# Two parts of the conditioning rows at a time beside the last o products, in matmuls of 512 columns

## The chip, the cores and the metric

The kernel runs on one core of one Trainium2 chip. Its engines each take their own list of instructions in order: TensorE (PE in the profile; its weight loads are PEld), VectorE (DVE), ScalarE (ACT), GpSimd (POOL) and SyncE (SP), which here issues the DMAs. Semaphores hold them together. The metric is the device time of one execution in microseconds (us), lower is better.

## The reference

One inference step of a two-layer streaming encoder, for a prompt of 1024 rows and a sample of 32 rows, with width D = 1024. Layer 0 mixes by an mLSTM with 4 heads, layer 1 by chunk-band attention; both have an MLP with a squared ReLU. What matters here is the conditioning: each layer makes six vectors of 1024 entries (shift, scale and gate, twice) from the conditioning vector c of the sequence, and applies them to its rows.

```python
def ada_mod(c, w, b):
    return jax.nn.silu(c) @ w + b
...
sh1, sc1, g1, sh2, sc2, g2 = jnp.split(ada_mod(c, p['w_ada'][l], p['b_ada'][l])[:, None, :], 6, axis=-1)
u = x * (1 + sc1) + sh1
...
x = layer_norm(ALPHA * x + (1 + g1) * y, p['ln_g'][l, 0], p['ln_b'][l, 0])
u = x * (1 + sc2) + sh2
```

w_ada is 1024 x 6144 for each layer. c is a single row for the prompt and one for the sample, so these products have two rows of output and read 4 MB of weights for each of the six parts. The mLSTM mixer ends with an output gate, `h * sigmoid(o_pre)` with `o_pre = u @ w_in[:, 2048:3072]`, and `h @ w_out`.

## The kernel before

The program is written as a sequence of stages on one core, in fp32 with operands split in a high and a low half where a matmul must be exact. Loops are unrolled when the program is built; a scheduler puts the instructions of each engine in a fixed order, with waits on semaphores where data or a buffer has to be free.

Work that is not the stage's own runs beside it as a task: a Python generator that is handed to `flow` (class Flow, lines 47 to 75). The stage calls `flow.tick()` after each of its own pieces, here with 1.0; a task that is marked `fine` is advanced until the waits that it yields have used up the tick. What the task emits then stands behind that piece in the program's order.

The stage that the change touches is the last one of the mLSTM layer: `o_proj([2, 3], after_o)` (line 864), which makes the output gate of heads 2 and 3. For each of three blocks of rows (384, 384 and 288) and each head it makes two products of 24 matmuls (`proj`, 8 blocks of the contraction with three matmuls each), so twelve products, each with a tick behind it. The products' matmuls are the lines 120 to 122 with the tile name o; the gate itself is made on ACT and DVE from the result (lines 450 to 453, 626, 628).

Beside it runs the task `ada_o` (lines 852 to 863). It computes four of the six parts of layer 1's conditioning (shift and scale of both halves of the layer, parts 0, 1, 3 and 4; columns 48, 56, 72 and 80 of the tile ada), which are first used in the next stages' norms. Each part is one call of `ada_rows`:

- `load` (lines 267 to 272): a block of 128 rows of w_ada, 1024 columns, 512 KB, by one DMA on SP. The tile comes from `mk`, the ring of four y buffers that the heads have left. Three loads are issued ahead.
- line 282: for each of the 8 row blocks k four matmuls, one for each quarter q of the columns. The stationary operand is the two conditioning vectors, padded to 32 columns; quarter q goes to the 32 output partitions from 32q on. A matmul in fp32 is two records in the trace, each with a weight load.
- line 286: the 32 x 4 rows of result are copied by ACT from the bank `ada` (one buffer) to a tile sada, from the ring tmp (three buffers).
- lines 288 to 297: they are transposed on PE and added with the bias into ada by DVE.

The yields of `ada_rows` are 2.5 steps ahead of the first block, a step ahead of each other block and ahead of the copy, and three steps ahead of the transposes. `ada_rows` also serves the key and value conditioning (line 1507), there with two parts at once from one tile.

Beside the same products `ada_l0` (line 792) makes parts of layer 0's conditioning on DVE from 512 KB loads of its own; its result needs the bank `ada` too (line 249, adas). The stage that follows loads its accumulators (acc, line 1053) into memory that pool A gives back, then multiplies by w_out_a (tile op_a).

Of the kernel before, what the change touches and what calls it, by code (L numbers as in the profile page):

```python
# [8 lines left out]
F32 = mybir.dt.float32  # L9
# [6 lines left out]
P = 128  # L16
D = 1024
# [60 lines left out]
def trunk_kernel(ctx: ExitStack, tc: tile.TileContext, a, o):  # L78
    nc = tc.nc
# [6 lines left out]
    def raw_tile(shape, name):  # L86
        return ring.tile(shape, F32, tag="raw", name=name, bufs=3)
# [62 lines left out]
    cs = cp.tile([P, KC, 32], F32, name="cs")  # L150
# [8 lines left out]
    def lng(i):  # L159
        return pt1[:, i * KC:(i + 1) * KC]  # L160

    def lnb(i):
        return pt1[:, 32 + i * KC:32 + (i + 1) * KC]
# [3 lines left out]
    def ada_part(l, i):  # L167
        return ada[:, l * 48 + i * KC:l * 48 + (i + 1) * KC, :]
# [18 lines left out]
    def bank(name):  # L187

        bank_n[0] += 1
        return (tpt, nmt, adat, mmt, tpt, nmt, mmt, mmt)[bank_n[0] % 8](name)  # L190
# [67 lines left out]
    wa, wk = a["w_ada"], a["w_ada_kv"]  # L258
    LA = 6 * D * D

    def ada_rows(src, off, gap, bases, step, mk, bank, ahead=1, mk2=None, mkt=None):

        m = len(bases)
        w = m * D // 4
        nm = bases[0]

        def load(k):
            raw = mk([P, m * D], f"rada_{nm}_{k}")
            row = src.ap[-2][0]
            nc.sync.dma_start(raw.rearrange("p (i c) -> p i c", i=m), bass.AP(  # L270
                src.tensor, src.offset + off + k * P * row, [[row, P], [gap, m], [1, D]]))
            return raw
        raws = [load(k) for k in range(ahead)]
        ps = None
        for k in range(KC):
            if k + ahead < KC:
                raws.append(load(k + ahead))
            raw = raws.pop(0)
            yield step if k else 2.5 * step
            ps = ps or bank(f"adap_{nm}")  # L280
            for q in range(4):
                nc.tensor.matmul(ps[32 * q:32 * q + 32, :w], cs[:, k, :], raw[:, q * w:(q + 1) * w],
                                 start=(k == 0), stop=(k == KC - 1))
        yield step
        sb = (mkt or tmp_t)([P, w], f"sada_{nm}")
        nc.scalar.copy(sb, ps[:, :w])
        yield 3 * step
        ps2 = (mk2 or mmD)(f"adat_{nm}")[:, :w]
        for b in range(w // P):
            nc.tensor.transpose(ps2[:, b * P:(b + 1) * P], sb[:, b * P:(b + 1) * P], ident)  # L290
        for i, base in enumerate(bases):
            nq = 4 // m
            nc.vector.tensor_tensor(
                ada[:, base:base + 8, :].rearrange("p (q b) j -> p q b j", q=nq),
                ps2.rearrange("p (b q j) -> p q b j", b=w // P, q=4)[:, nq * i:nq * i + nq, :, 0:2],
                pt2[:, base:base + 8].rearrange("p (q b) -> p q b", q=nq)[:, :, :, None].broadcast_to(
                    [P, nq, 8 // nq, 2]), op=ALU.add)

    def ada_fix(base, parts):

        for i, kind in parts:
            ap = ada[:, base + i * KC:base + (i + 1) * KC, :]
            if kind == "sc":
                nc.vector.tensor_scalar_add(ap, ap, 1.0)
            else:
                nc.vector.tensor_scalar(ap, ap, 1.0, 1.0 / ALPHA, op0=ALU.add, op1=ALU.mult)

    def combine(ni, g, b, sc, sh):

        for cnd in range(2):  # L310
            nc.vector.tensor_mul(comb[:, ni, :, 0, cnd], g, sc[:, :, cnd])
            nc.vector.tensor_mul(comb[:, ni, :, 1, cnd], b, sc[:, :, cnd])
            nc.vector.tensor_add(comb[:, ni, :, 1, cnd], comb[:, ni, :, 1, cnd], sh[:, :, cnd])
# [57 lines left out]
    A = A_cm.__enter__()  # L371
# [480 lines left out]
    def ada_o():  # L852
        def mk(shape, name):
            return A.tile([P, YL], F32, tag="y", name=name, bufs=4)[:, :D]

        def mkt(shape, name):
            return A.tile([P, 384], F32, tag="tmp", name=name, bufs=3)[:, :shape[1]]
        for i in (0, 1, 3, 4):
            yield from ada_rows(wa, LA + i * D, D, (48 + 8 * i,), 0.22, mk, adat, 3, nmt, mkt)
        ada_fix(48, [(1, "sc"), (4, "sc")])  # L860
        combine(1, lng(1), lnb(1), ada_part(1, 1), ada_part(1, 0))
        combine(2, lng(2), lnb(2), ada_part(1, 4), ada_part(1, 3))
    flow.add(ada_o(), fine=True)
    o_proj([2, 3], after_o)
    flow.finish()
# [71 lines left out]
    def mmD(name):  # L937
        return psum["p"].tile([P, 512], F32, tag="mm", name=name, bufs=psum["n"])
# [567 lines left out]
    def ada_early():  # L1506
        yield from ada_rows(wk, 0, D, (96, 104), 2.9, wc_tile, ada_bank)
        ada_fix(96, [(1, "sc")])
# [170 lines left out]
    for ti, pr in ((2, 0), (2, 1), (2, 2), (1, 0), (1, 1), (1, 2), (2, 3), (1, 3), (0, 3), (0, 2), (0, 1), (0, 0)):  # L1679
# [8 lines left out]
        for fc in (2 * pr, 2 * pr + 1):  # L1688
            g, r = fc // 2, 2 * (fc % 2)
            gp, e = g // 2, g % 2  # L1690
            ps = mmD(f"q_{fc}_{t0}")
            proj(ps[:, :n], n, ws[pr], fc % 2, lambda hl, k: UQ[ti][:, hl, k])
            for hd in range(2):
                for off, m, cnd in segs(t0, n):
                    if cnd == 0:
                        dst = QOT[ti][:, e, gp, 0:m // 64, (r + hd) * 64:(r + hd + 1) * 64]
                        src = ps[64 * hd:64 * hd + 64, off:off + m].rearrange("p (c i) -> p c i", i=64)
                    else:
                        dst = qo(16)[:, e, gp, (r + hd) * 32:(r + hd + 1) * 32]
                        src = ps[64 * hd:64 * hd + 64, off:off + m]  # L1700
# [17 lines left out]
    for i in range(4):  # L1718
        raw = raw_tile([P, 2, 512], f"raw_kv{i}")
# [356 lines left out]
```

## Time and profile before

| What | Value |
|---|---|
| median of 3 runs | 2340.04 us (2337.47 to 2340.95) |
| the profiled execution | 2338.54 us |
| its span, first to last instruction | 2336.8 us |
| granted TensorE clock over the span | 0.996 |
| bytes read from HBM, written | 329.65 MB, 95.46 MB |

In the views of the profile that follow, a row of a timeline has the start (us from the span's start), the time taken, the engine, the line of the kernel, the operation, output<-inputs by the program's tile names, the shape and the count; in square brackets stands how long the engine was idle before it, and what ended that. A row of groups has the busy time and the mean of one instruction in ns, then the idle time before. "SPq" is the issuing of DMAs by SyncE. A row of windows has the stretch, its length, the busy time of each engine with the number of its instructions, the granted clock, the DMA engines' busy share and GB/s. Records of matmuls overlap, so their distances from start to start tell more than their durations.

### The profile page before, as it was taken

How to read it: one execution, taken by the hardware profiler on the slowest of the kernel's cores; microseconds unless marked ns; L12 is line 12 of the kernel's file. 1: busy time of each engine (PE TensorE's matmuls, PEld its weight loads, DVE VectorE, ACT ScalarE, POOL GpSimd, SP SyncE). 2: the span in 40 equal slices, each digit the busy share in tenths (PEclk: the TensorE clock that was granted, in tenths of full speed). 3: DMA queues.
4: the chain of work that ended last, by engine and by line, in shares of the span. 5: the costliest groups of instructions: out<-in, count | busy, mean ns of one | idle time of the engine just before them, and what ended most of it. 6: DMA issues, size and time to landing. Idle time of an engine off the chain costs nothing. (4 is left out here: it accounts for less than half of the span.)

```text
span 2336.8 us, 44003 instructions
## 1 busy us (share of the span) xinstructions
PE 2279.9 (98%) x17266; PEld 2158.1 (92%) x17266; DVE 1823.1 (78%) x3480; ACT 1205.5 (52%) x2278; POOL 150.7 (6%) x309
## 2 busy tenths in 40 slices
PE   7999999999999999999999999999999999999997
PEld 5999998898899999999999877779999999999997
DVE  4899987686788888977886677755788888896777
ACT  4554445337844444333776766653784444433343
POOL 0111100000000000000000034420000000000021
PEclk9999999999999999999999999999999999999999
DMA  9422337747566679857641330042456667976753
GB/s 319 131 84 89 95 97 239 243 155 261 192 223 224 223 242 345 278 181 234 223 157 58 104 75 2 1 134 59 142 195 225 224 221 250 369 258 194 246 167 126
DMA packets 292703, 425.63 MB, mean 182 GB/s; under 512 B 17796, under 2 KB 174872, under 8 KB 291472
## 3 DMA queue, kind: packets, MB, share of 16 engines
q1 hardware_dynamic: 281648, 402.27, 52.9%
q10 hardware_dynamic: 10848, 20.55, 2.4%
q8 instruction: 136, 2.23, 0.4%
q14 instruction: 71, 0.58, 0.1%
HBM read 329.65 MB, written 95.46 MB: 182 GB/s over the span
## 5 line engine op out<-in xcount | busy, mean ns | idle before, releaser
L951 PE MATMUL dP<-t_P_None,w_P_None 128*128 128x256 f32 (+1 forms) x1280 | 365.3, 285 | 0.0
L949 PE MATMUL dP<-t_P_None,w_P_None 128*128 128x256 f32 (+1 forms) x1280 | 363.3, 284 | 0.3 <-DVE acd L1454 0.3
L950 PE MATMUL dP<-t_P_None,w_P_None 128*128 128x256 f32 (+1 forms) x1280 | 361.4, 282 | 0.0
L949 PEld LDWEIGHTS dP<-t_P_None,w_P_None 128*128 128x128 f32 x1280 | 241.2, 189 | 0.6 <-issue 0.5
L950 PEld LDWEIGHTS dP<-t_P_None,w_P_None 128*128 128x128 f32 x1280 | 241.0, 188 | 0.0
L951 PEld LDWEIGHTS dP<-t_P_None,w_P_None 128*128 128x128 f32 x1280 | 240.4, 188 | 0.0
L958 ACT CAST t_P_None<-rt_P_None 128x1056 fp32r<-128x1056 f32 x80 | 86.2, 1079 | 223.6 <-PE dP L951 165.1
L949 PE MATMUL e<-opB,wea 128*128 128x272 f32 (+1 forms) x512 | 146.4, 286 | 6.0 <-DVE sv L1224 3.2
L951 PE MATMUL dP<-t_P,w_P 128*128 128x256 f32 (+1 forms) x512 | 146.8, 287 | 0.1
L949 PE MATMUL dP<-t_P,w_P 128*128 128x256 f32 (+1 forms) x512 | 146.8, 287 | 0.0
L950 PE MATMUL dP<-t_P,w_P 128*128 128x256 f32 (+1 forms) x512 | 146.3, 286 | 0.0
L949 PE MATMUL uP<-opT,wb 128*128 128x264 f32 x512 | 145.7, 285 | 0.0
L951 PE MATMUL e<-opB,wea 128*128 128x272 f32 (+1 forms) x512 | 145.5, 284 | 0.0
L951 PE MATMUL uP<-opT,wb 128*128 128x264 f32 x512 | 145.5, 284 | 0.0
L950 PE MATMUL uP<-opT,wb 128*128 128x264 f32 x512 | 145.2, 284 | 0.0
L950 PE MATMUL e<-opB,wea 128*128 128x272 f32 (+1 forms) x512 | 145.0, 283 | 0.0
L959 DVE TENSOR_TENSOR t_P_None<-rt_P_None,t_P_None 128x1056 fp32r<-128x1056 f32 x80 | 100.2, 1253 | 45.7 <-ACT t_P_None L958 45.4
L958 ACT CAST wb<-rup 128x1024 fp32r<-128x1024 f32 x32 | 33.6, 1050 | 176.2 <-DVE rup L1177 176.2
L949 PEld LDWEIGHTS e<-opB,wea 128*128 128x128 f32 x512 | 96.2, 188 | 10.7 <-ACT sv L1222 4.3
L1158 ACT ACTIVATE h<-h 128x528 f32<-128x528 f32 x96 | 61.6, 641 | 71.9 <-DVE h L1271 71.9
L950 PEld LDWEIGHTS e<-opB,wea 128*128 128x128 f32 x512 | 96.2, 188 | 1.7 <-issue 1.7
L951 PEld LDWEIGHTS dP<-t_P,w_P 128*128 128x128 f32 x512 | 97.3, 190 | 0.4 <-DVE w_P L959 0.4
(419 smaller groups left out, 7492.1 us busy)
## 6 DMA issues: line engine op xcount, KB each, us to landing
rt_P_None<-h_d SPq DMA_DIRECT2D x80, 528.0 KB
rw_P_None<-in_w_down_dram SPq DMA_DIRECT2D x80, 512.0 KB
rada<-in_w_ada_dram SPq DMA_DIRECT2D x72, 512.0 KB
rup<-in_w_up_dram SPq DMA_DIRECT2D x64, 512.0 KB
rw_P<-in_w_down_dram SPq DMA_DIRECT2D x48, 512.0 KB
h_d<-h SPq DMA_DIRECT2D x30, 792.0 KB
rea<-in_w_up_dram SPq DMA_DIRECT2D x64, 256.0 KB
h_d<-t SPq DMA_DIRECT2D x30, 528.0 KB
```

Source lines behind the costliest of these rows:

```text
L949: nc.tensor.matmul(ps, wh, xh, start=start, stop=False)
L950: nc.tensor.matmul(ps, wh, xl, start=False, stop=False)
L951: nc.tensor.matmul(ps, wl, xh, start=False, stop=stop)
L958: nc.scalar.copy(op[:, 0], src)
L959: nc.vector.tensor_sub(op[:, 1], src, raw32(op[:, 0]))
L1158: nc.scalar.activation(dst, dst, AF.Relu)
```

## The change

`ada_o` now calls `ada_rows` twice instead of four times, each time for two neighbouring parts (0 and 1, then 3 and 4). A new argument `parts` gives it the weights of the two parts. A row block is then two tiles of 128 x 1024, each by a load of its own from the same ring of four y buffers, with one row block loaded ahead. The four matmuls of a row block have 512 columns each: quarters 0 and 1 read the first tile's halves, quarters 2 and 3 the second's. The step is 0.44 instead of 0.22. The copy sada has 512 columns and takes a y buffer instead of a tmp buffer. The call for the key and value conditioning goes without `parts` and is as before.

```diff
-    def ada_rows(src, off, gap, bases, step, mk, bank, ahead=1, mk2=None, mkt=None):
+    def ada_rows(src, off, gap, bases, step, mk, bank, ahead=1, mk2=None, mkt=None, parts=None):
 
         m = len(bases)
         w = m * D // 4
         nm = bases[0]
 
         def load(k):
+            if parts:
+                raw = [mk([P, D], f"rada_{b}_{k}") for b in bases]
+                for i in range(m):
+                    nc.sync.dma_start(raw[i], parts[i][k * P:k * P + P])
+                return raw
             raw = mk([P, m * D], f"rada_{nm}_{k}")
...
             for q in range(4):
-                nc.tensor.matmul(ps[32 * q:32 * q + 32, :w], cs[:, k, :], raw[:, q * w:(q + 1) * w],
+                nc.tensor.matmul(ps[32 * q:32 * q + 32, :w], cs[:, k, :],
+                                 raw[2 * q // 4][:, q % 2 * w:q % 2 * w + w] if parts else raw[:, q * w:(q + 1) * w],
                                  start=(k == 0), stop=(k == KC - 1))
...
         def mkt(shape, name):
-            return A.tile([P, 384], F32, tag="tmp", name=name, bufs=3)[:, :shape[1]]
-        for i in (0, 1, 3, 4):
-            yield from ada_rows(wa, LA + i * D, D, (48 + 8 * i,), 0.22, mk, adat, 3, nmt, mkt)
+            return mk(shape, name)[:, :shape[1]]
+        for i in (0, 3):
+            yield from ada_rows(wa, 0, 0, (48 + 8 * i, 56 + 8 * i), 0.44, mk, adat, 1, nmt, mkt,
+                                [wa[1][:, (i + r) * D:(i + r + 1) * D] for r in range(2)])
```

## The prediction

> **What bounds the kernel now.** The page comes first: its span, TensorE's share and the granted clock.
>
> ```profile
> span 2336.8 us, 44003 instructions
> PE 2279.9 (98%) x17266; PEld 2158.1 (92%) x17266; DVE 1823.1 (78%) x3480; ACT 1205.5 (52%) x2278; POOL 150.7 (6%) x309
> PEclk9999999999999999999999999999999999999999
> ```
>
> TensorE (PE) works through 98% of the span at full clock, so the change is worth what it adds to or takes from PE's line of work, plus any hole it makes there. Next, the groups by line from 372 to 440 us, the stretch of the last o products; the rows of L282 by itself; and PE's timeline there.
>
> ```profile
> L282 PE MATMUL adap<-rada,cs 128*32 128x256 f32 x256 | 17.4, 386 | 0.0
> L282 PEld LDWEIGHTS adap<-rada,cs 128*32 128x32 f32 x256 | 6.4, 109 | 6.5 <-issue 2.9 <-DMA rada<-in_w_ada_dram 1.2 <-PE o L121 0.2
> L282 PE MATMUL adap<-rada,cs x320: 379/379/617, 373.8 to 559.9; 128*32 128x256 f32 x128, 128*32 128x512 f32 x32
> L286 ACT COPY sada<-adap x5: 353/354/593, 387.7 to 565.8; 128x256 f32<-128x256 f32 x4, 128x512 f32<-128x512 f32 x1
> ```
>
> ```profile
> 373.85 1.50 PE L282 MATMUL adap<-rada,cs 128*32 128x256 f32 x24
> ...
> 381.48 0.34 PE L121 MATMUL o<-U,w_o 128*128 128x384 f32 x1
> 381.75 0.64 PE L282 MATMUL adap<-rada,cs 128*32 128x256 f32 x8
> 382.32 0.44 PE L122 MATMUL o<-U,w_o 128*128 128x384 f32 x1
> 382.60 0.34 PE L120 MATMUL o<-U,w_o 128*128 128x384 f32 x1
> 382.77 0.34 PE L121 MATMUL o<-U,w_o 128*128 128x384 f32 x1
> ...
> 391.52 0.33 PE L122 MATMUL o<-U,w_o 128*128 128x384 f32 x1
> 391.78 1.50 PE L282 MATMUL adap<-rada,cs 128*32 128x256 f32 x24
> 393.21 0.44 PE L120 MATMUL o<-U,w_o 128*128 128x384 f32 x1
> 393.49 0.34 PE L121 MATMUL o<-U,w_o 128*128 128x384 f32 x1
> ...
> 415.56 1.95 PE L282 MATMUL adap<-rada,cs 128*32 128x256 f32 x32
> ...
> 435.30 0.64 PE L282 MATMUL adap<-rada,cs 128*32 128x256 f32 x8
> 436.60 0.26 PE L249 MATMUL adas<-cx,sel 128*32 128x16 f32 x8 [0.67 <-ACT sada L286]
> 436.79 0.44 PE L290 MATMUL adat<-ident,sada 128*128 128x128 f32 x2
> 436.99 0.43 PE L120 MATMUL op_a<-U,w_oa 128*128 128x384 f32 x1
> ```
>
> The conditioning rows run as bursts between the o matmuls: one row block k (128 rows of w_ada, one part) is eight records, four column quarters in two passes. From the burst at 373.85 to that at 435.30 there are 17, holding 32 blocks (256 records). A burst of one block moves o's starts from 381.48 to 382.32, 0.84; one of three from 391.52 to 393.21, 1.69. So a block costs (1.69 - 0.84) / 2 = 0.43 us, and a burst, beside it, 0.84 - 0.43 - 0.17 (o's usual distance, 382.60 to 382.77) + 0.11 (the next distance is 0.28 instead of 0.17) = 0.35. Before, in all: 32 x 0.43 + 17 x 0.35 = 19.7 us, nothing of it hidden.
>
> Two more things are to be seen. Eight records of 379 ns fit into 0.64, so the four quarters run side by side. And the burst at 381.75 stands in the middle of a product, between an L121 and its L122. Each engine takes its instructions in an order fixed when the program is built; that order sets a block down, matmul by matmul, where its load is expected, and not at the end of a product. The 1.2 us of waiting for rada in five waits (no longer than the pauses that "issue" has elsewhere) say that this fits the real landings.
>
> The loads come last: SyncE's timeline, its waits, and two windows.
>
> ```profile
> 289.89 0.97 SPq L270 DMA_DIRECT2D rada<-in_w_ada_dram  x2
> 355.42 0.92 SPq L270 DMA_DIRECT2D rada<-in_w_ada_dram  x2
> 374.55 0.35 SPq L270 DMA_DIRECT2D rada<-in_w_ada_dram  x1
> 410.43 1.28 SPq L270 DMA_DIRECT2D rada<-in_w_ada_dram  x3
> 430.44 0.33 SPq L270 DMA_DIRECT2D rada<-in_w_ada_dram  x1
> 436.00 3.13 SPq L1053 DMA_DIRECT2D acc<-xsp  x2
> SPq L270 <- PE adap L282: 36.5, 17, 4.5
> 378.00:392.00 14.00, 14.00 (x104) 10.79 (x107) 4.61 (x11) 7.32 (x17) 0.00 (x0) 1.00 0.89 300
> 437.00:450.00 13.00, 13.00 (x77) 13.00 (x76) 12.93 (x45) 0.88 (x2) 0.00 (x0) 1.00 0.97 354
> ```
>
> Four loads of 512 KB wait in the four y buffers by 360 us; each further one is issued when a block has been used (36.5 us of SyncE's waits are for that). At 354 GB/s, the fullest window, a load takes 1.48 us; at 300 GB/s, 1.75. The three issued from 410.43 on are the last three blocks of the burst at 415.56, whose fourth starts 3 x 0.43 later, at 416.85: three loads landed in at most 6.4 us, so there is at most 6.4 - 3 x 1.48 = 2.0 us beside the transfers; I take 1.5.
>
> **The change, part by part.**
>
> Matmuls. 128 of 256 columns become 64 of 512. Row block k is now two parts wide, and the form is already in the trace (the key and value conditioning):
>
> ```profile
> 536.13 0.29 PE L951 MATMUL e<-opB,wea 128*128 128x272 f32 x1
> 536.35 1.06 PE L282 MATMUL adap<-rada,cs 128*32 128x512 f32 x8
> 537.35 0.39 PE L949 MATMUL e<-opB,wea 128*128 128x272 f32 x1
> 537.58 0.29 PE L950 MATMUL e<-opB,wea 128*128 128x272 f32 x1
> 537.70 0.29 PE L951 MATMUL e<-opB,wea 128*128 128x272 f32 x1
> ```
>
> 537.35 - 536.13 - 0.12 + (0.23 - 0.12) = 1.21 for the burst, less 0.35 for the burst itself: 0.86, twice 0.43. Streaming: 16 x 0.86 = 13.8, as before. **0.**
>
> Bursts. The stretch goes in twelve products of 24 matmuls, with one tick of 1.0 after each. Before, the steps of 0.22 put 3, 4 and 1 blocks behind three products in a row, four times over. With 0.44 (the first step 1.1) they are 0, 3, 2, 2, 1, 0, 0, 3, 2, 2, 1, 0. Two buffers are now one block, so only blocks 0 and 1 of each pair lie ready; they go together, and 2 to 7 come as they land: 1 + 6 bursts a pair, 14 in all, if a block stays whole. 3 x 0.35: **-1.0.**
>
> Halves. A block's four quarters now read two tiles, 0 and 1 the first part, 2 and 3 the second, with a load each, and the loads land 1.48 to 1.75 us apart. Quarters 0 and 1 are ready first, and where PE has reached neither the block's place nor its second load, the order sets them down alone, with o matmuls behind them (as at 381.75), and 2 and 3 later. No row shows a half. From one side it costs nothing more: 0.43 for half the columns. From the other it costs a whole block again: the four quarters run side by side, so the 0.86 of a whole block are the time that each quarter takes for its own 512 columns in two passes, whether two quarters run or four. I take that end, the one to which the 617 ns of a single record are nearer. Each split block then costs 0.86 more.
> By the Trainium skill, TensorE: Matmul & The Clock Gate, "Measured speedup vs the span model", packed tiles last as long as one matmul and about 4 ns for each further tile; by that a half costs a whole as well, and the sum is the same.
>
> How many split? I walked the twelve products with 1.5 us plus the transfer for a load. Block 2 of a pair is freed for loading when block 0 is done; its parts land 3.0 and 4.5 us later, the second past the end of the product that runs meanwhile (24 x 0.17 = 4.1). Blocks 2, 3 and 4 of both pairs split so; 5 to 7 are held back by the ticks more than by loads, at 1.48 us a load. That is 7. At 1.75 us, more of the blocks 5 to 7 split too: 10. I take 8. Halves of neighbouring blocks often share a burst, so I count 3 more bursts, not 8: 8 x 0.86 + 3 x 0.35 = **+7.9** (bounds 0 and 10 x (0.86 + 0.35) = 12.1).
>
> Loads. 32 of 512 KB as before, on the same queue, in the same four buffers; the first (374.55) comes one product later and none is started while products 6 to 8 run. Behind product 8, PE has four products of 288 columns (24 x 0.13 each), 7 blocks and 6 bursts ahead of the last block: 12.5 + 6.0 + 2.1 = 20.6. The twelve loads need 0.86 + 0.2 + 1.5 + 12 x 1.48 = 20.3, or 23.6 at 1.75. With the halves PE needs 3 to 4 us more and the loads are hidden: **0**; without them PE would wait 0 to 3.0.
>
> Copies and the end. Two copies of 593 ns for four of 354 on ACT, which has room. The transposes stay eight. At the end PE waits for the copy (0.67 at 436.60), which is 0.24 longer: **+0.2.** That sada leaves the tmp buffers for a y buffer holds back one load of the second pair until its transposes, in a stretch in which no block is due. The acc loads (436.00) wait for the last block and move with it, as does PE.
>
> Sum: -1.0 + 7.9 + 0.2 = +7.1. The profiled execution took 2338.54, of which the span is 2336.8; 2345.6 on its terms. It lies 1.5 under the median of 2340.04, so I forecast **2347** for the median. 4.7 us (0.2%) is about what a measurement of this kernel can tell from no change.
>
> **The rivals.**
>
> Blocks stay whole (the other side). If both loads are expected at nearly one time, or a half isn't set down alone, the sum is -1.0 + 0.2 + a wait at the end of 0 to 3.0, I take 1: 2340.3, not slower. It decides at less than 5 splits. For it: at 391.78 three blocks stand together. Against: 381.75 shows a block placed matmul by matmul, for a later load. Chance 0.27.
>
> Waits. If the fixed order is too early for the second load, PE stops: up to 1.75 us for each of 12 blocks, 21 us, 2361. Against it are the five short waits (1.2 us) before. Chance 0.07. A smaller share of it lies in the range.
>
> Fewer instructions are worth something. Were the weight loads not hidden, 128 fewer of 109 ns would be up to 14 us less; against it, 0.86 is twice 0.43, with no remainder per instruction. Whole blocks and a gain of 5 us: 2335. Chance 0.05.
> The Trainium skill, TensorE: Matmul & The Clock Gate, "LDWEIGHTS (loading the stationary operand)", gives columns / 1.2 ns, here an estimated 27 ns: 3.4 us less for 128 if none were hidden. The trace speaks against it.
>
> **How the numbers follow.** Halves 0.61, whole blocks 0.27, waits 0.07, fewer instructions 0.05. Halves give +4.4 (6 splits in the same 14 bursts, -0.8 with them) to +11.3 (10 splits, each with a burst of its own). The range reaches from whole blocks with no wait (2338.5 - 0.8 + 1.5 = 2339.2, and 1 us of measurement, 2338) to ten splits (2338.5 + 11.3 + 1.5 = 2351.3, and 2 us of waits, 2353). Halves fall within 4.7 us with 0.09 of their 0.61, whole blocks with 0.25 of 0.27: slower 0.61, same 0.34, faster 0.05.
>
> **What would show it.** In the changed profile, L282 in bursts of four records of 592 to 617 ns with o matmuls between, some 8 pairs of them, and about 17 bursts; the first op_a near 444 instead of 436.99. Wrong, if all bursts are of eight or sixteen, or if L282 waits for rada for more than some 3 us.

## The result, and the profile after

| | before | after |
|---|---|---|
| median (runs) | 2340.49 us (4) | 2353.18 us (4), 2351.86 to 2354.83 |
| ratio, 95% interval | | 1.0054 [1.0042, 1.0066] |
| the profiled execution | 2338.54 us | 2352.45 us |

The changed kernel is 12.7 us slower. The forecast was 2347.0, slower, with a range that ends at 2353: the sign and the mechanism came out as put, the size is nearly twice too small.

The page's lines that answer to those of before (line 282 is now 287, 286 is 292, 290 is 296):

```profile
span 2350.7 us, 43742 instructions
PE 2293.2 (98%) x17138; PEld 2157.3 (92%) x17138; DVE 1825.0 (78%) x3480; ACT 1207.0 (51%) x2276; POOL 151.5 (6%) x309
PEclk9999999999999999999999999999999999999999
```

128 matmul records fewer (17138 for 17266), yet PE is busy 13.3 us longer, at the same clock. Where, two windows show. They run from the first o matmul of the twelve products to the first op_a, restricted to the tile adap (columns: stretch, its length, then busy time and number for PE, PEld and ACT). Before:

```profile
368.71:436.99 68.28, 17.36 (x256) 6.37 (x256) 1.42 (x4) 1.00 0.75 252
```

After:

```profile
367.46:450.43 82.97, 28.12 (x128) 4.21 (x128) 1.15 (x2) 1.00 0.64 207
```

The stretch is 14.7 us longer, and the row matmuls alone take 10.8 us more with half the records. In the execution profiled after, it begins 1.25 us earlier (367.46 for 368.71), so the first op_a comes 13.4 us later. The rest of the kernel keeps its time: from the first op_a to the last instruction it is 1899.8 us before and 1900.2 after. The DMA share falls from 0.75 to 0.64, so the stretch isn't short of bandwidth.

The groups of the tile adap after (in the manner of before's rows: count, three durations in ns with the usual one in the middle, first and last start):

```profile
L287 PE MATMUL adap<-rada,cs x128: 592/593/617, 376.8 to 447.4; 128*32 128x512 f32 x128
L292 ACT COPY sada<-adap x2: 567/577/587, 409.5 to 449.2; 128x512 f32<-128x512 f32 x2
```

And PE's timeline after. It is cut to the bursts and the o matmuls on which a distance is read:

```profile
376.78 1.93 PE L287 MATMUL adap<-rada,cs 128*32 128x512 f32 x16
383.38 1.05 PE L287 MATMUL adap<-rada,cs 128*32 128x512 f32 x4 [1.15 <-DMA rada<-in_w_ada_dram]
...
387.75 0.33 PE L121 MATMUL o<-U,w_o 128*128 128x384 f32 x1
388.01 1.05 PE L287 MATMUL adap<-rada,cs 128*32 128x512 f32 x4
388.99 0.44 PE L122 MATMUL o<-U,w_o 128*128 128x384 f32 x1
389.27 0.34 PE L120 MATMUL o<-U,w_o 128*128 128x384 f32 x1
389.45 0.34 PE L121 MATMUL o<-U,w_o 128*128 128x384 f32 x1
389.62 0.34 PE L122 MATMUL o<-U,w_o 128*128 128x384 f32 x1
389.89 1.05 PE L287 MATMUL adap<-rada,cs 128*32 128x512 f32 x4
...
419.84 1.93 PE L287 MATMUL adap<-rada,cs 128*32 128x512 f32 x16
...
424.92 1.05 PE L287 MATMUL adap<-rada,cs 128*32 128x512 f32 x4 [0.45 <-DMA rada<-in_w_ada_dram]
...
446.87 1.12 PE L287 MATMUL adap<-rada,cs 128*32 128x512 f32 x8
449.83 0.26 PE L249 MATMUL adas<-cx,sel 128*32 128x16 f32 x8 [1.84 <-ACT sada L292]
450.02 0.66 PE L296 MATMUL adat<-ident,sada 128*128 128x128 f32 x4
450.43 0.42 PE L120 MATMUL op_a<-U,w_oa 128*128 128x384 f32 x1
```

What to see: only the two ready pairs of blocks (x16) and the very last block (x8) are whole. Every other one, 11 of 16, is split into two bursts of four records, 22 in all, so there are 25 bursts instead of 17. Between the halves of one block stand only four o matmuls (five of 288 columns later on). A half moves o's starts from 387.75 to 388.99, 1.24; less o's usual 0.17, plus 0.11 for the slower next distance (389.27 - 388.99 = 0.28), that is 1.18 us.

Why do so many split? A split block seems to hand its split on: each of its halves gives its buffer back when it is done, and only then is the load issued that goes into that buffer. After the halves at 383.38 and 385.26 SyncE issues the two loads of the block after next at 384.48 and 386.36, 1.9 us apart, and that block comes in two bursts again (392.66 and 394.54). In the run whole, below, the same two loads are issued at 389.06 and 389.49. That this is what keeps the later blocks split is a reading of these rows; no run tests it by itself.

So the 14.7 us come apart as 11 x 1.18 = 13.0 for second halves, -1.0 for the bursts saved otherwise (14 instead of 17, 0.35 each), 1.6 for the waits on rada (1.15 and 0.45), and 1.2 at the end (a wait on the copy of 1.84 for 0.67): 14.8.

### The profile page after: what moved, and what is told of

Its sections match the earlier page's. It is cut to its first block, busy times and chain, and to the rows that moved or that the text cites. A ratio compares the mean times of both kernels' runs of the same rounds, so it can differ in the third digit from the quotient of the medians.

```text
span 2350.7 us, 43742 instructions
## 1 busy us (share of the span) xinstructions
PE 2293.2 (98%) x17138; PEld 2157.3 (92%) x17138; DVE 1825.0 (78%) x3480; ACT 1207.0 (51%) x2276; POOL 151.5 (6%) x309
## 5 line engine op out<-in xcount | busy, mean ns | idle before, releaser
L1165 ACT ACTIVATE h<-h 128x528 f32<-128x528 f32 x96 | 61.7, 642 | 72.2 <-DVE h L1278 72.1
```

The source lines that it names most:

```text
L1165: nc.scalar.activation(dst, dst, AF.Relu)
```

## The experiments

The theory, "halves": the cost is that a block served by two loads is set down in two places, each of which costs what the whole block costs. The rivals: the second load makes PE wait; the place of sada, which the change moved too, is at fault; there is a cost in the 512-column form itself. All ratios are to the kernel before on the same chip. "Stretch" is that of the windows above, in the one execution that was profiled; before and after it, executions differ by some us too (from the first op_a to the end, 1897.2 to 1903.9 us over these runs), so a stretch and a median need not move by the same amount.

| kernel | median, before | ratio [95%] | stretch | bursts |
|---|---|---|---|---|
| before | | | 68.28 | 17 |
| the change | 2353.18, 2340.49 | 1.0054 [1.0042, 1.0066] | 82.97 | 25 |
| whole | 2343.09, 2339.05 | 1.0014 [1.0004, 1.0023] | 72.8 | 13 |
| across | 2343.01, 2339.05 | 1.0016 [1.0007, 1.0025] | 73.3 | 26 |
| sada_y | 2341.16, 2339.05 | 1.0013 [1.0003, 1.0022] | 72.2 | 26 |
| two_queues | 2353.17, 2339.05 | 1.0058 [1.0043, 1.0073] | 83.6 | 14 |
| act_queue | 2345.26, 2338.62 | 1.0029 [1.0017, 1.0041] | 74.9 | 14 |
| change_rc | 2351.87, 2338.62 | 1.0062 [1.0047, 1.0078] | 82.4 | 25 |
| whole_rc | 2343.88, 2338.62 | 1.0021 [1.0012, 1.0030] | 72.6 | 13 |
| groups_of_six | 2336.10, 2338.62 | 0.9985 [0.9976, 0.9994] | 65.9 | 7 |

### whole: the changed kernel, with no block split

Quarters 0 and 1 also depend on the block's second load; nothing else differs from the change.

```diff
-                    nc.sync.dma_start(raw[i], parts[i][k * P:k * P + P])
+                    last[k] = nc.sync.dma_start(raw[i], parts[i][k * P:k * P + P])
...
-                nc.tensor.matmul(ps[32 * q:32 * q + 32, :w], cs[:, k, :],
+                mm_ = nc.tensor.matmul(ps[32 * q:32 * q + 32, :w], cs[:, k, :],
...
+                if parts and q < 2:
+                    tc.add_manual_dep(mm_.ins, last[k].ins.name, mybir.DependencyInfo(
+                        mybir.DependencyClass.Sync, mybir.DependencyReason.DATA), reason="whole block")
```

> The changed kernel, but quarters 0 and 1 of a row block also wait for the block's second load, so that the order can only set whole blocks down. Loads, buffers, ticks and matmuls stay those of the change. Theory of the halves (a split block streams its 512 columns twice, 0.86 us more, and makes a burst more, 0.35): 14 bursts instead of 25, none of four records; 11 x 0.86 + 11 x 0.35 = 13.3 us less than the change, less what PE then waits for loads (1 to 4 us): 2341 to 2344 us, L282's successor in bursts of 8 or 16 records only. Rival, the loads (two buffers a block, first load one product later): nothing in them is changed, so it stays within 3 us of 2353, with the time in waits for rada. Rival, sada in a y buffer: stays at 2353.

PE's timeline of whole around one block:

```profile
391.17 0.34 PE L121 MATMUL o<-U,w_o 128*128 128x384 f32 x1
391.44 1.06 PE L288 MATMUL adap<-rada,cs 128*32 128x512 f32 x8
392.43 0.44 PE L122 MATMUL o<-U,w_o 128*128 128x384 f32 x1
392.71 0.34 PE L120 MATMUL o<-U,w_o 128*128 128x384 f32 x1
```

Eight records move o's starts by 1.26, where four records moved them by 1.24. The second two quarters cost 0.02 us if they start with the first two, and 1.18 if they come later. This is the core of the case, in rows of one form, each between an L121 and an L122 of the same products. By the Trainium skill, TensorE: Matmul & The Clock Gate, "Measured speedup vs the span model", packed tiles take one matmul's time and about 4 ns for each further tile; two further tiles in two passes are an estimated 16 ns, with which the 0.02 us agree.

With no block split the stretch is 10.2 us shorter than the change's. It is still 4.5 longer than before's, and whole's waits say why, for the most part:

```profile
PE adap L288 <- DMA rada<-in_w_ada_dram: 4.1, 2, 2.6
PE adas L249 <- ACT sada L296: 0.7, 1, 0.7
```

-1.4 for four bursts fewer and +4.1 of waits are +2.7 of the 4.5. Most of the other 1.8 is the clock. From the last 0.5 us of the longest wait on, ahead of the last block, the granted clock is 0.50 for 6.8 us (PE's timeline, then a window, in which 0.50 is the clock):

```profile
439.24 1.94 PE L288 MATMUL adap<-rada,cs 128*32 128x512 f32 x8 [2.56 <-DMA rada<-in_w_ada_dram]
```

```profile
438.70:445.50 6.80, 5.56 (x28) 3.82 (x29) 3.21 (x22) 0.95 (x2) 0.00 (x0) 0.50 0.06 7
```

The last block's eight records take 1.94 instead of 1.06. From its start to the first op_a (442.88), without the wait for the copy, whole takes 2.95 us and the change 1.72, so 1.2 of the 1.8. Behind the stretch it costs another 1.2: the first nine distances of op_a take 2.87 us, before 1.66. whole_rc, below, has the same: a wait of 2.28, then 0.50. But a wait of 2.94 in two_queues has no such stretch behind it, so what makes the clock fall isn't shown.

whole's ten executions fall apart by the clock over their span. The five with 0.995 or 0.996 took 2338.46 to 2342.17 us, the five with 0.991 to 0.994 2344.01 to 2347.24. Only one of them, of the second five (2344.24, 0.992), was profiled. So the median of 2343.09 seems to hold a part that is the clock's and not the blocks'. The prediction's rival of whole blocks allowed a wait of 0 to 3.0.

### across: the change's loads, without the lost concurrency

Each part's tile feeds all four quarters with 256 columns, as before; the second part accumulates in a bank of its own, and so the copy becomes two of 256 columns (not shown). Loads, order of loading, steps and buffers are the change's.

```diff
...
-            for q in range(4):
-                nc.tensor.matmul(ps[32 * q:32 * q + 32, :w], cs[:, k, :],
-                                 raw[2 * q // 4][:, q % 2 * w:q % 2 * w + w] if parts else raw[:, q * w:(q + 1) * w],
+            for q in range(4 * m if parts else 4):
+                i, q = divmod(q, 4)
+                if parts and not k and q == 0:
+                    pss.append((bank if i == 0 else tpt)(f"adap_{bases[i]}"))
+                nc.tensor.matmul(pss[i][32 * q:32 * q + 32, :256] if parts else ps[32 * q:32 * q + 32, :w],
+                                 cs[:, k, :],
+                                 raw[i][:, q * 256:q * 256 + 256] if parts else raw[:, q * w:(q + 1) * w],
...
```

> The changed kernel's two loads a block, ticks, buffers and copy size, but each part's tile feeds all four quarters with matmuls of 256 columns, as before the change (the second part into a PSUM bank of its own). A block may still be split, but a half then keeps four quarters side by side. Theory of the halves: the number of bursts stays near 25, each half costs 0.43 instead of 0.86, so 11 x 0.86 = 9.5 us less than the change: 2342 to 2346 us. Rival, that only the number of bursts counts: no gain, 2350 to 2354. Rival, the loads: within 3 us of 2353.

PE's timeline of across, at a burst that again stands by itself:

```profile
387.02 0.34 PE L120 MATMUL o<-U,w_o 128*128 128x384 f32 x1
387.29 0.64 PE L291 MATMUL adap<-rada,cs 128*32 128x256 f32 x8
387.86 0.44 PE L121 MATMUL o<-U,w_o 128*128 128x384 f32 x1
```

One load, one burst, as in the change, and even one burst more (26). But a load's worth of rows moves o's starts by 0.84 instead of 1.24. The stretch is 9.7 us shorter than the change's; 22 half blocks x (1.24 - 0.84) are 8.8, and the shorter waits on rada (1.1 for 1.6) and at the end, less one burst more, give the rest. So it isn't the number of bursts, and not the time of the loads, that makes up the change's loss: it is that half the columns of work occupy PE as long as all of them.

### sada_y: the change's other edit by itself

The kernel before, with sada in a y buffer.

```diff
-            return A.tile([P, 384], F32, tag="tmp", name=name, bufs=3)[:, :shape[1]]
+            return mk(shape, name)[:, :shape[1]]
```

> The kernel before with one part of the change alone: the copy sada (256 columns) takes a y buffer instead of a tmp buffer. Theory of the halves: nothing is split, one load of each part waits until the transposes, 2339 to 2343 us. Rival, sada in a y buffer is what costs: 2347 us or more.

The prediction costed this edit at nothing. In the kernel before it is worth 4 us of the stretch; the medians differ by 2.1 us, and the profiled executions by only 0.7 (2339.20 and 2338.54), since this one was shorter elsewhere. SyncE's waits in sada_y (us in total, times, the longest) show three loads held back until the transposes (L290) have given sada's buffer back, a wait that before doesn't have:

```profile
SPq L270 <- PE adap L282: 40.0, 22, 3.5
...
SPq L270 <- PE adat L290: 2.7, 3, 0.9
```

The order sets the blocks down in 26 bursts instead of 17: 9 x 0.35 = 3.2 us. That the held-back loads are what spreads them is how I read it; no run separates the two. The last 1.0 is at the end, in PE's wait for the copy (0.67 before):

```profile
PE adas L249 <- ACT sada L286: 1.7, 1, 1.7
```

ScalarE's timeline in sada_y reads there

```profile
438.02 0.44 ACT L452 ACTIVATE og<-og 128x288 f32<-128x288 f32 x1
438.98 0.44 ACT L626 ACTIVATE og<-og 128x288 f32<-128x288 f32 x1 [0.53 <-DVE og L453]
439.33 0.35 ACT L286 COPY sada<-adap 128x256 f32<-128x256 f32 x1
```

and that of before

```profile
435.84 0.44 ACT L451 ACTIVATE og<-og 128x288 f32<-128x288 f32 x1
436.19 0.35 ACT L286 COPY sada<-adap 128x256 f32<-128x256 f32 x1
436.44 0.44 ACT L452 ACTIVATE og<-og 128x288 f32<-128x288 f32 x1
```

The copy's length is the same. What differs is its place: before it goes into the middle of the gate; here it stands behind the whole gate, with a DVE step in it. The change has this too (ScalarE's timeline after):

```profile
447.89 0.44 ACT L458 ACTIVATE og<-og 128x288 f32<-128x288 f32 x1
448.86 0.44 ACT L632 ACTIVATE og<-og 128x288 f32<-128x288 f32 x1 [0.53 <-DVE og L459]
449.21 0.57 ACT L292 COPY sada<-adap 128x512 f32<-128x512 f32 x1
```

So most of the 1.2 us at the end of the change is an order on ScalarE, and 0.22 the longer copy (0.57 for 0.35).

### change_rc and whole_rc: sada elsewhere in the changed kernels

If sada's buffer costs 4 us before, does it in the change? Both kernels put it into the buffer rc, which nothing else uses there.

```diff
-            return mk(shape, name)[:, :shape[1]]
+            return rc_tile([P, YL], name)[:, :shape[1]]
```

> The change with one part undone: sada in the unused buffer of rc instead of a y buffer. Theory of the halves: the blocks are split as before, 25 bursts, so at most 1 to 2 us less than the change, 2350 to 2353 us. Rival, that sada in a y buffer (which alone cost the kernel before some 2 us) is a large part of the loss: 2348 or less.

> The run with whole blocks, and sada in the unused buffer of rc instead of a y buffer, so that no load of the second pair waits for the transposes. The run with whole blocks kept 4.8 us of PE's waits. If sada's place makes them: the last of them (2.6 and 0.7 us near the end) shrink, 2339 to 2341 us. If they come from two buffers a block and the loads' own pace: 2341 to 2344, as with sada in y.

Neither differs from its counterpart: 82.4 us of stretch for 83.0, 72.6 for 72.8, with the same 25 and 13 bursts. Both medians lie where they were expected (2350 to 2353 and 2341 to 2344). The splits are there already, and the loads come one block at a time whatever sada does. The waits of whole_rc for rada stay as they are in whole, so they don't come from sada's buffer:

```profile
PE adap L288 <- DMA rada<-in_w_ada_dram: 4.1, 4, 2.3
```

The two costs don't add: the 4 us of sada_y are no part of the change's 14.7. That holds for the end too: in change_rc the copy stands behind the gate as in the change, and from the last block's burst to the first op_a it is 3.57 us for 3.56.

### two_queues and act_queue: both loads at once

The second part's load is issued by GpSimd (two_queues) or ScalarE (act_queue, with nc.scalar), beside the first on SyncE.

```diff
-                    nc.sync.dma_start(raw[i], parts[i][k * P:k * P + P])
+                    (nc.sync, nc.gpsimd)[i].dma_start(raw[i], parts[i][k * P:k * P + P])
```

> The changed kernel, with the load of a block's second part issued by GpSimd instead of SyncE. Both loads can then be expected at about one time, and the order keeps the blocks whole if it is the expected landings that split them. Theory of the halves: bursts of 8 or 16 records only, 13 us less on PE, and, since the 16 DMA engines are shared and the loads land no sooner, waits of PE for rada of some us in their place: 2341 to 2350 us. Rival, that quarters are split for another reason than the landing: bursts of four records as in the change, 2350 or more.

> The change, with the load of the second part issued by ScalarE instead of SyncE (the run with GpSimd kept the blocks whole and lost 11 us in waits for loads instead). If those waits were made by the order expecting the loads of two queues side by side while the same DMA engines carry both: whole blocks, and 8 to 12 us of waits for rada again, 2348 to 2354 us. If GpSimd's way of issuing was slow: waits under 4 us, 2340 to 2345 us.

In both, all blocks are whole (14 bursts, the prediction's number), though the dependences are the change's; nothing is set down between the halves, even where PE waits between them. Only the engine that issues a load differs, so this fits an order that sets a half down where it expects its load, and a whole block where it expects both together; the expectation itself stands in no trace. What comes of it is that PE waits instead. two_queues took 2353.17 us, more than the 2341 to 2350 that I had expected; act_queue, with 2345.26, has the waits of the first of its two expectations and nearly the time of the second. The waits of two_queues:

```profile
PEld adap L287 <- DMA rada<-in_w_ada_dram: 15.7, 10, 3.2
PE adap L287 <- DMA rada<-in_w_ada_dram: 11.1, 7, 2.9
```

Those of act_queue:

```profile
PEld adap L287 <- DMA rada<-in_w_ada_dram: 8.1, 12, 1.5
PE adap L287 <- DMA rada<-in_w_ada_dram: 3.8, 4, 1.2
```

PE's row is too low here, since a record's end is modelled and covers a short wait. Act_queue's burst at 383.02 is an example, in PE's timeline and then in PEld's:

```profile
383.02 2.02 PE L287 MATMUL adap<-rada,cs 128*32 128x512 f32 x8
```

```profile
383.02 0.14 PEld L287 LDWEIGHTS adap<-rada,cs 128*32 128x32 f32 x4 [0.29 <-DMA rada<-in_w_ada_dram]
383.99 0.14 PEld L287 LDWEIGHTS adap<-rada,cs 128*32 128x32 f32 x4 [0.83 <-DMA rada<-in_w_ada_dram]
```

The burst is 0.96 longer than an undisturbed one (1.06), and PE's row has no wait for it. With PEld's rows the stretches nearly add up: -1.0 for three bursts fewer, 15.7 and 8.1 of waits, and -0.7 in both, where adas no longer waits, give +14.0 (measured 15.3) and +6.4 (measured 6.7). In two_queues the clock is at 0.50 for 3.4 us, from the burst at 426.32 on, which goes toward the rest. So the rival "waits" names a real price, which an order can pay in place of the splits; the change itself paid 1.6 of it.

Why GpSimd's loads cost twice ScalarE's wasn't taken further. The Trainium skill, DMA: Bandwidth & Descriptors, "Issuing engine by pattern", says that loads issued by SyncE or ScalarE are generally faster than GpSimd's; 15.7 against 8.1 us of waits go with it.

### groups_of_six: fewer bursts without the change

If a burst costs 0.35 and a split 1.18, the kernel before can be bettered in the other direction. Single parts and 256 columns as before, but the 32 row blocks go in groups of six behind every second product, out of six buffers (the four y buffers and two that lie idle there), with the parts alternating between two banks.

```diff
-        for i in (0, 1, 3, 4):
-            yield from ada_rows(wa, LA + i * D, D, (48 + 8 * i,), 0.22, mk, adat, 3, nmt, mkt)
...
+        for b in range(6):
+            load(b)
...
+        for g in range(6):
+            yield 2.0 if g else 1.0
+            for b in range(6 * g, min(32, 6 * g + 6)):
+                rows(b)
+                if b + 6 < 32:
+                    load(b + 6)
...
```

> The kernel before with its single parts and 256 columns, but row blocks in groups of six behind every second product, in six row buffers (the four y buffers, and the buffers of qkp and rc that the heads have left), and the row sums in two PSUM banks in turn, so that a part's end doesn't wait for the copy of the one before. Theory of the halves and bursts (0.43 a whole block, 0.35 a burst): about 7 bursts instead of 17, 10 x 0.35 = 3.5 us less, and the 0.67 us at the end gone: 2335 to 2337 where before has 2339, a ratio of 0.998. Rival, that bursts cost nothing by themselves or that the waits for six loads at once take it back: 0.9995 to 1.002.

It beats both kernels: 2.5 us under before, with an interval that excludes 1, though barely. PE's timeline of groups_of_six:

```profile
395.46 0.33 PE L122 MATMUL o<-U,w_o 128*128 128x384 f32 x1
395.72 2.80 PE L874 MATMUL adap<-rada,cs 128*32 128x256 f32 x48
398.45 0.44 PE L883 MATMUL adat<-ident,sada 128*128 128x128 f32 x2
```

Six blocks in one burst, 2.80 us long: 0.43 for each beyond the first's 0.64 are 2.79. There are 7 bursts, so ten are saved: 3.5 us by the prediction's 0.35, less 0.6 for a wait on rada, is 2.9, and the stretch is 2.4 shorter. The kernel also has more buffers, a second bank and another order at its end, so the 2.4 is not a measurement of the bursts alone.

## Why the direction was right and the size wrong

**What bounds it**: right. PE stayed at 98% and full clock, the rest of the kernel kept its time, and the end moved by the 13.4 us that the first op_a moved (436.99 to 450.43).

**Matmuls, 0**: right. A whole 512-column block moves o by 1.26, twice 0.43 and the burst's 0.35, less the 0.11 that shows in the next distance but plus o's own 0.17.

**Bursts, -1.0**: right. Of the 25, 14 are what whole blocks would need.

**Halves, +7.9**: the mechanism is right, the term mis-sized. It measures 11 x 1.18 = 13.0 us. Two choices in it failed. First, the count: "I take 8" of "7" and "10", where 11 of the 12 late blocks split. The prediction had let blocks 5 to 7 be held back by the ticks, so that both loads would have landed. In the change every late block follows the loads, 388.01 and 389.89 and so on, two halves for each block to the last but one. The prediction left out that a split block gives its two buffers back 1.9 us apart, so that the next loads into them are issued 1.9 us apart too. Second, the bursts: "Halves of neighbouring blocks often share a burst, so I count 3 more bursts, not 8". None shared. Each second half paid its 0.35 as well, 11 x 0.35 = 3.9 for 1.05. The count is 2.6 (3 x 0.86) and the bursts 2.8 of what was missing. The price of a half (a whole block's 0.86; 1.18 - 0.35 = 0.83 measured) was the part with no row in the trace before, and it held. Of the signs that were named, the bursts of four records came, with 592 to 617 ns, but 11 pairs of them instead of 8, 25 bursts instead of 17, and the first op_a at 450.43 instead of 444.

**Loads, 0**: nearly. "With the halves PE needs 3 to 4 us more and the loads are hidden" left out the first load behind each ready pair; PE waits there, 1.15 and 0.45. In whole, where that cover is gone, the waits are 4.1, above the 0 to 3.0 given; and behind the longest of them the clock was at 0.50, for which the sum had no term.

**Copies and the end, +0.2**: off by 1.0. The copy's length was right; it was its place in ScalarE's order, behind the gate, that was not thought of.

**sada's move, nothing**: wrong as a statement on the edit (4 us of stretch alone, sada_y), without effect on the sum, since the blocks were split anyway (change_rc).

**The rivals**: whole blocks cost 4 us in the median (whole), not nothing; whole's five executions at a clock of 0.995 or more lie around this rival's 2340.3 (2338.46 to 2342.17), the other five above it. "Waits" is real in two_queues, not in the change. Fewer instructions were worth nothing: whole has 128 records fewer and is not faster.

**The range**: its upper end was ten splits and 2 us of waits, 2353. Eleven splits, the waits and the end go 0.2 beyond it.

## What to carry to other kernels

Here two of four column quarters took PE as long as all four (1.24 and 1.26 us): before giving such a group of matmuls two sources, ask whether both will be there at the same moment, and count a missing partner as a whole further pass. In this kernel's fixed order, work that followed its loads followed every single load, and work done in halves gave its buffers back in halves; bounds for such a count belong at "all of them" unless a row shows otherwise. And when a tile moves to another ring, look at what that ring's next user waits for, and where the tile's producer stands in its own engine's order, even where the buffer itself looks free.

## What the runs showed of the hardware

- Two column quarters of 512 columns in fp32 move the o matmuls by 1.24 us, four by 1.26. That the second two are free to within 0.02 us was closer than expected.
- A record of PE's can cover a wait: PE's row of waits shows 3.8 us in act_queue where PEld's shows 8.1, and the distances of the o matmuls side with PEld.
- The same 512 KB loads, issued by GpSimd beside SyncE instead of by ScalarE, left PE's weight loads waiting 15.7 us instead of 8.1. The cause stays open.
- In whole, the granted clock fell to 0.50 for 6.8 us in the last 0.5 us of PE's wait of 2.56 us; eight 512-column records then took 1.94 us instead of 1.06, and op_a's matmuls stood 0.32 us apart instead of 0.17. whole_rc shows the same behind a wait of 2.28, two_queues 3.4 us of it behind one of 1.66, and none behind one of 2.94. What ties the two together isn't shown.
